# Last block of a fused GLA and RWKV-7 trunk: some scalings go from ACT and DVE to POOL, and the written-out order is another one

## The chip, the cores and the metric

The kernel runs on one core of a Trainium2 chip. The metric is the device time of one execution in microseconds. The core's engines are PE (TensorE; its weight loads are listed apart as PEld), DVE (VectorE), ACT (ScalarE) and POOL (GpSimd); SP (SyncE) issues the DMAs.

## The reference

One layer of a decoder trunk, batch 1, 4096 tokens, width 1024, all in float32. Cut to what matters:

```python
h = _rmsnorm(x, norm_w)
u = h @ w_in                                   # one input projection for both groups
gla_out  = rmsnorm_per_head(gla_chunked(q, k, v, log_a)) * gla_norm_w * silu(gg)     # 512 wide
rwkv_out = (groupnorm(rwkv7_scan(r, decay, k, v, kk, a)) * ln_w + ln_b + bonus) * silu(rg)   # 512 wide
merged = concatenate([gla_out, rwkv_out], axis=-1)          # 1024 wide
x = x + merged @ w_out
return _rmsnorm(x, final_norm_w)
```

The RWKV-7 recurrence is `S_t = S_{t-1} (diag(w_t) - kk_t^T (a_t kk_t)) + v_t^T k_t`, `y_t = S_t r_t`, for 8 heads of 64.

## The kernel before

**Tiling.** Everything is held transposed: features on the 128 partitions, tokens along the free axis. The 4096 tokens go in 8 blocks of `TB = 512`. A tensor of width 1024 is `KT = 8` row tiles of 128 x 512.

**Products in float16.** Each big product is made of float16 pairs: a scaled float32 tile becomes a high half (the scaled value rounded to float16) and a low half (what the rounding left). The weight is split in the same way, and three products are added in a bank of PSUM: high by high, weight high by low, weight low by high. `proj` writes that order; within it the row tiles go from 0 up, and the matmul of row tile 0 starts the bank. A step of PE that the code calls `both` is two matmuls, for the two halves of the output's partitions.

**Streams.** Generators emit the work of each stage for each block: the input norm, the weights' splitting, the RWKV preparation (a), its inverse (i), its chunk recurrence (c, and e for the very last unit), GLA (g), projections (p) and the output (o). They record 23,821 steps, each an instruction or a fixed pair with its engine, its data dependences and a number.

**The order is written out.** `ORDER` is a packed list with one rank for every step. The kernel issues the steps by rank, as far as the dependences allow (a heap of the steps whose predecessors are out), and this fixes each engine's own sequence, SP's queue of DMAs too. `STARTS` and `COUNTS` give every step a planned start, which decides how the streams interleave while the steps are recorded. Both lists were computed ahead of time and are data here.

**The last block's output, `out_last`.** Of the eight row tiles of the last merged block, the first six (`K0 = KT - 2`) are ready before the last two pairs of RWKV heads are. So the output projection of the six runs first:

- The largest absolute value of the six gives one scale, `am` (tile `oaml` in the profile).
- `scaled(k, a, ts)` makes the high half of row tile `k` on ACT into `mh[k][:, 0]` and the low half on DVE into `mh[k][:, 1]` (tiles `x` in the profile; their sources are `mgg` and `mgr`). The low half reads the high half.
- `proj(w, mh, "o", K0)` runs for each of the eight output row tiles `n`, with weights in `wr`, `wg` and `wo` in turn, three of them at a time on PE. DVE adds the residual into `part[n]`.

Meanwhile the last recurrence goes on: PE, ACT copies (`us`, `uv`, `gt`, `vt`) and DVE (`sv`) in a chain, between the projection's matmuls. The last two row tiles come in two halves of 256 tokens. For each half `i`: the two tiles are scaled, `last_mm` adds their products to `part[n]`, ACT squares it, PE sums the squares over features, DVE does a Newton iteration for the inverse root (`nva`, `nta`, `nyg`), PE spreads the result over the partitions, ACT copies it to `rb`, and each `part[n]` is multiplied by the final weight and that factor. For `n < 2` ACT multiplies by the weight beforehand and POOL by `rb`; for the others DVE does both in one instruction that reads the factor in PSUM. SP then stores each of the eight tiles, 128 KB each.

POOL's other work is the inverse of small triangular matrices (`Tc`, `tm`), sums of squares (`xacc`) and fills.

In the profile nearly all instructions carry the line of the helper that issued them (L849, or L910 for the paired matmuls), so steps are told apart by their tiles.

Of the kernel before, what the change touches and what calls it, by code (L numbers as in the profile page):

```python
# [17 lines left out]
U8 = mybir.dt.uint8  # L18
AF = mybir.ActivationFunctionType
ALU = mybir.AluOpType  # L20
# [4 lines left out]
P = 128  # L25
DM = 1024
KT = 8
TB = 512
TH = TB // 2
C = 64  # L30
# [12 lines left out]
DP = 0.15  # L43
DO = 0.3
SO = 0.3
DL = 0.6
# [11 lines left out]
    "c-q}v2bdjY)t)=IZ{KWsZzQBa5)vRFB!SSRBTYa-0Vx841qI}%hzJ&>SpWe+iedp3ML`6l7XkUD2}B?eY9N7-w!3%#Ihpr(-#z)J+}#cG{CS?q-FxrcnQy*wzH{F5o^!@~o|g%ZTyQ+y)zy{3``#Rl!SS)+2rkz("  # L58
    "Ab5Ql*ZoKES_zI~@OL&ie4O)fyvlbs2gk<2`~MAIHws=K3|{91uOow_Gx+<q;K<=V9l_rP{JkdlyM({xI$6^uy_cWR_UD6hT7%ai^ci1kaB$><<DHnk`VHD8?VX9w#-k1Lw><wT!Etr){h;9WNPPbN;QbD0=c%~<"
    "@ZgZ=nh+chqy3|T<E`NDrr=fj>hE~o8NqQU+CL3{OFQ}p$7{jgZD{|Z;O}zqIyE@Xr03`t9CePd)W7rS^E~yx{9SK8@1!v*(=~k@SseBFd;mV*GC1y`F>1i8%!5bK&hhAb`TdCC_%qIz`;EnQWv<*x&-DuamcD+I"  # L60
    "K9@e-0PWCr74Z8k&D&|1Q*u0B317d0{_^Sfa$Jnx9)sWR6C7^`f3L*6U*nj+Q>jg3g8xpY_t}K`+Arq2oa6T`HLm613Ewx#y32(3k$xGCK6IU1LVxG!v*zGf75wn4GU?@d^h_n1H!|*<<9WUsoPVy!23#*g^QElq"
    "!nNgIy9DR|E_i(|xW$RV>$mW#b7pby{Z^UkJ@*QZofBl?&|b>O4TEEA%$?_PFPYD+)GyjkB8!gh1KI3D7W9RT&(?VUV?p~j#owDjmOX)I@~M3yFWZC9CqSN6u!mG|?gfy0DqEV+ma$k{KKf0sRSJH%8uRnE;P`i?"
    "de8olCH*nyhSPHmr@0^XtViHp+oEkbTz4AgnC<%v#ygK|=BYn)f0~TzoE7{%ya(f3PI>MJ!S(y0t+Jnd5BqK%_6TXqX;{x0tm&bUjlU0$9nJGK^>7~5)83+cxBP3wK5_^8w-d5bzFUEN&rZ0u$hzs6Ynxziah<2~"
    "Y8uwR%%fSs>%W56<@j6fE3*7g!Rz)qFFM2V%9C#Km|xrT*Y(kQ)bam1&9x8n_(E`e7JaGr|3=V1j|Ba42-g4Q*q2Yj-1AAs%kdeRTfukJu(tjh{C#6^d@lHVN$`4;8NX%0`<5E!Sv|>yEXHg)zJD+H`%n1ppy2Ow"
    "g4dr1uips{)%9jVPVoAbYurz|XJ3t@>ImbY7ha9IB6`I2Mn4#7ey{p-t@kZs-x*4J(t*J-F*u$H-v2Z>-jBHMP&4ncSWnj^v||`##|JpC0nh0}4*57|GWJRN_mkk5NIIA5c0Ub{J<a_li7XC|Iq1uU!T0j|TqV9;"
    "#hCB%Df&`m#|dcP1;KHA@c#FZVcU`Jp|WR>;J<lj({||d>CkU$*@tuV`Ihv#+EKdCTob%L37zzb;J&*BuOjQN#ksq8g`fG3@$xap+VJ=4;M|Ylo`(c~Z)NmS)%SORd=lOGYr*SP!RsH<p3l*E%&1{a7h~qK9jk_z"
    "YssE641d2H(dSun?OOIXKBh*@vv$mnF~K3a(jKHA$#G1?J<i5?MXX;r7SQ*b<M(3Ui(L3Y@b^QoXY~5FC(N^klyYl*?JooH`g4a~wG5w$jMxPIum*Y~pL=rfz~^Mb{&}DDNFCcPg5#TX{hax|tk+kA??<H2e;Y8T"
    "RHtc-Id@=ih@SNl_P%AXZ++-Mosd~7BW3=bYW4s*_q1N<^78v{n|>YM$75Jb`2O%-USIa${ei3OQ%Se~*?oJpnO~(8<E($rgZw)S`g?}t;~kK5hX=<%`b{nNnC!oYVZKbndM=QhQ#r9M_PQIPlU_i&^~m7ZAO<gB"
    "omlmdm9WS7+}4CX@d<ZH>icPsc`QFhQX76_t}_n%`d9FLz8O3HY$){&V-iDfzr4W)f9a4JwH}2S{G--&@<1?P&*B;P$G+48nIQPV%hdLvuy?wkTW^TJABBGUM_f~EmoF1mSHw7Uk<4iz`KWsGAZp)UIPaF=^E!NA"
# [2122 lines left out]
```

## Time and profile before

| what | us |
|---|---|
| median of 3 runs | 2143.97 |
| lowest and highest run | 2140.78, 2145.99 |
| the profiled execution | 2141.45 |
| its span in the trace | 2139.7 |
| PE busy | 2092.8 |
| DVE busy | 1611.2 |
| ACT busy | 1276.9 |
| POOL busy | 898.7 |

The span is from the first instruction to the last; the execution's own time has 1.75 us around it. Busy time is a sum of instructions' durations; PE's are pipelined and their ends modelled, so starts are the safer thing to read on PE. A row of the timeline gives start, duration, engine, line, operation, `out<-in`, shapes and count, and in square brackets the engine's idle time before it with the work that ended it. Consecutive instructions of the same kind are merged into one row with their number behind the x.

### The profile page before, as it was taken

The numbers are of one execution on the slowest core, as the hardware profiler recorded it, in microseconds if no ns is written. First come the engines' busy times: TensorE is split into PE (matmuls) and PEld (weight loads), VectorE is DVE, ScalarE is ACT, GpSimd is POOL, SyncE is SP. The second block draws the span as 40 slices with busy tenths as digits, with TensorE's granted clock in tenths as the row PEclk, the third lists the DMA queues.
The fourth block names the chain that finished last, engine by engine and source line by source line (L and its number), as shares of the span: only waits on it lengthen the run. The fifth ranks groups of instructions, "written<-read, shape, count | busy, mean of one in ns | idle before, by whom it ended". The sixth has DMA issues, their size and how long they took to land. (4 is left out here: it accounts for less than half of the span.)

```text
span 2139.7 us, 69390 instructions
## 1 busy us (share of the span) xinstructions
PE 2092.8 (98%) x27936; PEld 1358.5 (63%) x27936; DVE 1611.2 (75%) x3531; ACT 1276.9 (60%) x3361; POOL 898.7 (42%) x2365
## 2 busy tenths in 40 slices
PE   7999999999999999999999999999999999999998
PEld 5656675666755657557576567656676565755566
DVE  8889988668775787678776776757877488676776
ACT  7678786465644656455755457545575465654563
POOL 3663344561353541636433264442434534444500
PEclk9999999999999999999999999999999999999999
DMA  6758656465344643455534554345634465444442
GB/s 177 232 154 260 212 176 184 129 193 169 93 132 130 200 142 113 122 152 181 150 98 123 168 177 142 105 127 184 180 99 118 135 189 164 112 109 137 140 126 90
DMA packets 273703, 322.33 MB, mean 151 GB/s; under 512 B 129844, under 2 KB 135140, under 8 KB 273380
## 3 DMA queue, kind: packets, MB, share of 16 engines
q1 hardware_dynamic: 273380, 317.89, 49.8%
q8 instruction: 219, 3.59, 0.7%
q14 instruction: 104, 0.85, 0.1%
HBM read 272.74 MB, written 45.05 MB: 149 GB/s over the span
## 5 line engine op out<-in xcount | busy, mean ns | idle before, releaser
L910 PE MATMUL bank<-x,wr 128*64 128x512 f16 (+1 forms) x6732 | 834.4, 379 | 3.0 <-ACT wr L849 1.5
L849 POOL TENSOR_TENSOR tm<-Tc,f 128x60 f32<-128x60 f32 (+24 forms) x961 | 330.0, 343 | 584.4 <-DMA f<-nd 511.4
L910 PEld LDWEIGHTS <-wr 128*64 128x64 f16 x6732 | 367.0, 111 | 258.2 <-issue 17.2
L910 PE MATMUL bank<-x,wg 128*64 128x512 f16 x3180 | 397.1, 380 | 2.0 <-DVE amW L849 1.4
L849 POOL TENSOR_TENSOR Tc<-Tc,tm 128x60 f32<-128x60 f32 (+24 forms) x961 | 361.6, 376 | 73.8
L910 PE MATMUL bank<-x,wo 128*64 128x512 f16 x2760 | 327.5, 380 | 0.0
L849 POOL TENSOR_TENSOR xacc<-xacc,xr 128x256 f32<-128x256 f32 x196 | 154.4, 813 | 317.4 <-ACT xr L849 193.9
L849 DVE SCALAR_TENSOR_TENSOR sv<-ch,PC,psd 64x64 f32<-64x64 f32 x434 | 122.6, 282 | 217.8 <-PE ch L910 193.0
L910 PEld LDWEIGHTS <-wg 128*64 128x64 f16 x3180 | 174.7, 110 | 130.7 <-issue 3.8
L910 PEld LDWEIGHTS <-wo 128*64 128x64 f16 x2760 | 150.3, 110 | 115.5 <-issue 1.2
L910 PE MATMUL bank<-wg,x 128*64 128x256 f16 x3072 | 197.6, 273 | 2.2 <-DMA wg<-wdr 2.0
L849 ACT COPY us<-ch 64x64 f32<-64x64 f32 x496 | 102.0, 206 | 146.8 <-PE ch L910 123.1
L910 PEld LDWEIGHTS <-x 128*64 128x64 f16 x3264 | 174.7, 110 | 15.5 <-DMA wg<-wdr 2.5
L849 ACT COPY uv<-ch 64x64 f32<-64x64 f32 x496 | 102.0, 206 | 93.1 <-PE ch L910 86.1
L849 ACT ACTIVATE psd<-sv,PC 128x128 f32<-128x128 f32 x248 | 98.7, 398 | 61.6 <-DVE sv L849 54.8
L849 ACT ACTIVATE sa<-bank,mu_s 128x512 f32<-128x512 f32 x104 | 71.3, 686 | 60.4 <-PE bank L910 52.0
L849 DVE COPY_PREDICATED DD<-mc,bank 64x512 f32<-64x512 uint8 x128 | 92.9, 729 | 4.4 <-PE bank L849 2.0
L849 DVE COPY_PREDICATED Nb<-mc,bank 64x512 f32<-64x512 uint8 x128 | 93.0, 730 | 3.3 <-PE bank L849 0.9
L910 PEld LDWEIGHTS ch<-us,Nb 128*64 128x64 f32 x992 | 66.4, 137 | 40.3 <-ACT us L849 10.8
L910 PEld LDWEIGHTS ch<-uv,bk 128*64 128x64 f32 x992 | 67.2, 137 | 38.7 <-ACT uv L849 5.7
L910 PEld LDWEIGHTS ch<-sv,DD 128*64 128x64 f32 x992 | 66.5, 137 | 35.6 <-DVE sv L849 9.3
L910 PE MATMUL ch<-us,Nb 128*64 128x64 f32 x992 | 71.6, 223 | 5.2 <-ACT us L849 5.2
(367 smaller groups left out, 3550.4 us busy)
## 6 DMA issues: line engine op xcount, KB each, us to landing
wr<-wdr SPq DMA_DIRECT2D x254, 256.0 KB
wg<-wdr SPq DMA_DIRECT2D x182, 256.0 KB
xr<-in_xT_dram SPq DMA_DIRECT2D x176, 256.0 KB
wo<-wdr SPq DMA_DIRECT2D x116, 256.0 KB
f<-nd SPq DMA_DIRECT2D x128, 128.0 KB
x<-in_wt_dram SPq DMA_DIRECT2D x29, 512.0 KB
wdr<-wo SPq DMA_DIRECT2D x17, 512.0 KB
rn<-bcda SPq DMA_DIRECT2D x64, 128.0 KB
```

The source lines that it names most:

```text
L849: put(t0, self.name, d, lag, cols, tiles, tab, outs, ins, lambda: f(*a, **kw))
L910: nc.tensor.matmul(x, lhsT=l, rhs=y, start=start, stop=stop)
```

## The change

Three things change.

1. In `scaled`, the high halves of row tiles 1, 3 and 5 of the first six are made by POOL with a `tensor_scalar`; the other highs stay on ACT, all lows on DVE.
2. In the final scaling, `n < 2` becomes `n < 2 + i`: in the second half (`i = 1`) three tiles go over ACT and POOL, and DVE has five. This makes one step more, 23,822.
3. `ORDER` is a new list. `STARTS` gains one entry and `COUNTS` counts it.

```diff
             def scaled(k, a, ts):
-                S.activation(mh[k][:, 0, ts], mgt[k][:, ts], AF.Copy, scale=am[:, a:a + 1])
+                if k < K0 and k % 2:
+                    G.tensor_scalar(mh[k][:, 0, ts], mgt[k][:, ts], am[:, a:a + 1], None, ALU.mult)
+                else:
+                    S.activation(mh[k][:, 0, ts], mgt[k][:, ts], AF.Copy, scale=am[:, a:a + 1])
                 V.scalar_tensor_tensor(mh[k][:, 1, ts], mgt[k][:, ts], am[:, a:a + 1], mh[k][:, 0, ts], ALU.mult, ALU.subtract)
...
                 for n in range(KT):
-                    if n < 2:
+                    if n < 2 + i:
                         S.activation(part[n][:, ts], part[n][:, ts], AF.Copy, scale=pkt[:, PK_FN + n:PK_FN + n + 1])
                         G.tensor_tensor(part[n][:, ts], part[n][:, ts], rb, ALU.mult)
                     else:
...
-COUNTS = (... ('o', 2545), ...)
+COUNTS = (... ('o', 2546), ...)
```

The packed list `ORDER` is left out of the diff. Decoded, the sequence of ACT around the first six highs is, before: uv, uv, gt, gt, high 0, vt, high 1, high 2, vt, high 3, high 4, us, us, high 5; after: uv, gt, gt, uv, high 0, high 2, vt, vt, high 4, us, us. POOL's new sequence there is high 1, high 3, high 5; DVE's lows go 0, 1, 2, 3, 5, 4 in place of 0, 1, 2, 4, 3, 5.

More of the change, by code (lines that the diff above doesn't have):

```diff
@@ new lines @@
+    "qmE0~Z4}<Wgmc%%n#jMu281fKdMfDL$DHZ!FTv|E!8y6$^<$v(6?m@Y!D}&iU4e1SI*g|=jSl`h-9cN~2wLk(pyzDD=Pe1pACd5Vmy9)2x#nnEH>Mfgn`6zM5;|QJOz4R+xuA&-d?&xj;oND#u@*i*IXM5^;PoNw"
+    "g(5z0!x(b7MhpJlIXM3p!Ryn(ElvzxzZ$%L9^VP?c`^8YyG*zTWe;p6>z2R^ht<g=g{G#1c3unaC3Dsu9Ljq-XwC+Lp6cbxzTssVTszaxhwDDVi#EdF<AdXc;Qd|T6MVjpxtWMHFGGgN{*%8i2j5fLZ6&%|jy+Yt"
+    "XR=14%i+YyoL(rjf_cniju!^++wu1Z8p~Ml3)l1I@j4GQv@Pzdv?@ILY{z=(dbZO3lh+w^&Ujqs>!69Y8t1(+<#`_j*YChsMJ8Mnyk7@%It=pYl;9W!nrs1|mhnCu96Orl8_-X*qw=PNab6!B2Y`R-K3|S|ubXhK"
@@ new lines @@
+    "0idA=gY&0Bwz%Yff%c^G=8eEF7U6H@4IrnL`bbYel<Q$#_47yk{@qJy*Hd55aOf-_#UXU^JItlZ%5wq*=x@R6{=sKI3SRFIUVjz5ei1r~eLk7fhd_s)3Xb0ff8P=uM?rtN)zI7`(m9fjX2_)i=^wqI3)NYE3!UxI"
+    ";J7IG`+LFb*PxHeIUCR($kKkl7kjn8<}z>ifyk?yuqTA}ucvv)L0{qDuOFeyrx{}#^xo&8uN(?q{1kZaq6j%O+OenPci&BrTSIXycAO`4@Lcfuw$Oi{1zlYl9HY!!jR}rjgX21L9a-Nq!DH8f9FqC@d$~4wny+yU"
+    "W!%RRt&~B_LhrLMKkXQ|oWEu8-`3@D&Ub<?KN@==Y40m7sxGbHO~vPOZ&|;|crSDKv*7jT!K={MUxE|%!hZS$_U{JJm3%`#S;)!J&>gZke-oVZN!UCcW}G?bRp$lAQNcMEK*s$B-yc%0=<Cz^VGoT?p#xjGSK0Gw"
@@ new lines @@
+    "!kiE6gFLgxRQkJQY*^KMJ`FypI>{*!eE$@TH;3nF01Yt@ku{%>{c{C)Rv9*meD<4uvi)5$xIeC=b99?yoD0FL#2%c4z1j(W!RK8TJn&~T;oj@Tvx{Cc4)*-a;PsrCd1$9KDy5)5u{&jdzlgbxqZ{=X<nhWn;c{Fj"
+    "gYV?^5<Ii|HL{SIY3V)c_(nhK4<q{Un@{xdUP{ON1+PB{UUw^pK7yp*S(*5uS^tI<_sw9x3N3v<cs(t6y`1*svf%GWKsytHV{?bUjIR}S$R3>ydHFiglTS9V{QYsz=k++}28{29;MgTNHcRjq<c<FMKAvS##GY`;"
+    "BpJ_}2|T5MebNXUMD9HZuWRCSSyR;^I&keK?C<lT&nvAiBcG2?GH8&w?-Z<S7xc<OxX)3JwW;-J#?c=((EY)pJqBOm-te~xA9xqG+xuRHm$lIPZ9p_4>n{Gt&w@Y7?{CC4dtpnL$TvEGWO|<VRWtFLxwzMzI7j!%"
@@ new lines @@
+    "hD66qL%$<B*v`=TKS&0xM|8}5|Bs|!FDKrZ$6OyAJf!$ieu4XlE^|b1Tphd@Ki~w+2h+wF%+I={$BcqqEZ_e#czrK{e$%Y;nh~GN`fU_k|L^2GlsTA<dwwNCN7)*-)(x<Ic7R^H(#IJbgW=OE&|1jf2a>L+>*ey%"
+    "tV4S+XP&hQ`shU12%F(t{qDlx#Fu(PKfa7@Q+$7B3LQ2R;p=E19d<e7oZ4NVz~{mXb^|Tv$Q~8H+E2h+E`<+apWyGqG1o_cK3Hb%Cj2<Kxaa~$_Ehs1%NrL2zZL)Pjll_<_EdZeS@Uc;$Nv6&@Y}0#?nLNgo#YFb"
+    "^L{Vy@yxyCKPzHibYiWi!xy4sodkOKq1*6%TOn^`?Zk)rx1Nd*pJ}=W`%>>+Ft+~opy9Ewb?yX@n1JtfETZR6!W=)2HPY*iGV}Bd(a8k*Zis^}{s7+7OFVnBIp+%UGZerR`1?y}ZiUXij&U52K(9mk!9V&G`4r^!"
@@ new lines @@
+    "7SJ%$&tS*?KZ3^4PV+nzHm*F2tjWH?aauXqj*&fdrR)V03v$`MLO+)W#|goCGFPX<p12NUm_hU+@3${kbRgAR7i2zKzf|Tw<PX#1=i=)Y8HK&2F*>2gYr8{UTCc7!-F)^)owi(u%K6}UHCV%AGNBB<2t20@*<<ys"
+    "UeX7eB6J$ouNx!u=`86rt)xfl8j22`%~bgDv*0Ub>|@rag;#!=-isc-9rlRYO>2QZ*(Pr_&o$OOOP=)pcA|Uc-<@P94kSHVjvay@ZUbMG=s?@!_a_mb=Vv}0`%}jF6#2F~an0YR@Iki6eAnuTB|bwspbuSrBJ5dt"
+    "{{x(NAn~omSPS);4tK<VdF@ZZTz(hhzY(t|2giI|Lv<CA7q1YFx%9DuvDwu3mW5oLhtG}xZRL%B!NoJy#P8(q&CTA*M$oy{4F{3z)-fF*K1;+k)_}d-VDwbc15d~J=V83oM=>a3KF$X(I0Syti)C-8;0>aq&%|7|"
@@ new lines @@
+    "8GC9O)_xYraT_Z=E_nY<{5=bCl(%qB5j=1Va1Y`mof~}d#h&o{M$&2S34Zf@!g%9o{%~4fvBxF8vx)Kh%bvJCSd6nVHa~&}vJP3CA#6vE_DLS&Qkl0E&iiHX-(JDJ&cb>|#TQ578sgWQ0v-QYv9Idj>v@W)sSe#~"
+    "zF$9u?3hKk4L$Z0{RNneWAK^yU@jmZNLt(3+I}*w3&CS8o<RTp9L}+FJ_}lFP2rmz<DjKoWX-^DK8?@BzjMQqa8F$m{Cxs+Y2lqSgZE3w_PQOqX#?r3N09IL=dewuV%)bv#^y2hM<Ey1!};gt-F%znrrMITFrU8-"
+    "HtYq3&^DL(ydikMUm@JfGN)$;?>8%iI(rFpy*ACC*p)jGU48|2`dIi12ATaa6`$!Gyqute=4;T`{D{5cL-&_^4l(pAJa#VDpcnC%9LauuT}ts`;RO?e_b<Voc^|Rx4`EZNO}(3AzxYJI1@QHSgj;awTLt=Ul1`{="
@@ new lines @@
+    "u9%{mvG;mmBhSY7_uzSbq9IG;f~C3?^t(Z?+h^K9xP^N4VewsweEBu@!YsswJ0KH<9_})8+JrU8g60@UHUfSp!R>tspU=iR4u>u%*ZgS=U)$6{hq_h|Ch)@zVT(26H+#}v7zuxkTzeq#Cws3AgZ~~ahx&-#_ek)X"
+    "mHtZjD0ip<FVI!T8jVkZ@9d_1<BHuj5v@vG@fO6X_Q3uV-`hcW-WjB$mEj{-oudbTPx=qpjjQ_@n(+O&OsGHf(!V=ags)p=Dwu%cYPNG<0X}!7Zzx!#T&AKgjHvV4MZ{b!&8qGze;<Z@CUo^BiDLjOvNb-xHo>k;"
+    ";~$VY-K8hwfoEpI{dOsMjL^9F;?E*|Sa?G@IB#%w82>&x(|2ElUh~s2_)WzHUTOAQGwBSXw~PIFQUc!^iRWq|pZfsl1ig?0Z#(YONdBEskPVwa|JoO8vJuwl`y}(kZV+DidhljNPiQA+h;J%wtAAio@ZUY%;qQO-"
@@ L366 @@
+    "Aqwt#KwHnkdxk*vyD<Wvbbr{Mxf*&=i?GA}Kc^=cG5"
 )
```

363 lines of the change are left out of this document (170 added, 193 removed).

## The prediction

> **What bounds the kernel now.** I read the page first: its busy shares say which engine to look at, and its slices whether that holds at all times.
>
> ```profile
> PE 2092.8 (98%) x27936; PEld 1358.5 (63%) x27936; DVE 1611.2 (75%) x3531; ACT 1276.9 (60%) x3361; POOL 898.7 (42%) x2365
> ```
>
> PE leaves 2139.7 - 2092.8 = 46.9 us of the span idle, and nothing but a part of that can be won while its work stays as it is. The view by stretches says where it lies (columns: stretch, length, then the busy time of PE, PEld, DVE, ACT and POOL with their instructions, PE's granted clock, DMA share, GB/s).
>
> ```profile
> 0.00:100.00 100.00, 82.44 (x962) 55.92 (x964) 85.43 (x235) 71.81 (x140) 47.78 (x102) 0.97 0.65 199
> 100.00:2000.00 1900.00, 1884.78 (x25084) 1213.57 (x25080) 1421.38 (x3001) 1135.31 (x3014) 827.60 (x2218) 1.00 0.51 151
> 2000.00:2040.00 40.00, 36.35 (x512) 26.49 (x509) 32.82 (x74) 20.28 (x55) 20.51 (x44) 1.00 0.41 125
> 2070.00:2080.00 10.00, 8.24 (x96) 4.91 (x94) 7.87 (x22) 9.52 (x30) 0.00 (x0) 1.00 0.77 199
> 2080.00:2124.00 44.00, 44.00 (x686) 31.29 (x683) 26.84 (x87) 15.97 (x54) 0.00 (x0) 1.00 0.21 67
> ```
>
> The change touches 2070 to 2080 (idle 10 - 8.24 = 1.76 us) and what comes after 2124. Between them PE is busy 44.00 of 44 us, so whatever PE gains before 2080 moves the end by as much, and an ACT or DVE step made shorter there gains nothing by itself. In the chain that ended last, the first stretch shows who holds PE back.
>
> ```profile
> 2073.56 0.73 ACT x L849
> 2074.33 0.41 PE bank L910 x2
> ...
> 2074.90 0.85 ACT x L849 x2
> ...
> 2076.00 1.34 ACT x L849 x2
> ...
> 2077.82 0.73 ACT x L849
> 2078.60 2.03 PE bank L910 x20
> ```
>
> The x rows are the high halves of the six row tiles, all made by ACT. The first releases PE at 2074.33, the last at 2078.60; from 2078.60 the chain stays on PE. POOL does nothing in that time, and ACT is busy for 9.52 of the ten microseconds.
>
> **The first edit: three highs on POOL.** ACT's highs cost 718 ns each; between them stand the copies of the last recurrence.
>
> ```profile
> L849 ACT ACTIVATE x<-mgg,oaml 128x512 f16<-128x512 f32 x4 | 2.8, 718 | 0.1
> ...
> 2072.65 0.42 ACT L849 COPY uv<-ch 64x64 f32<-64x64 f32 x2
> 2073.10 0.44 ACT L849 COPY gt<-bank 64x64 f32<-64x64 f32 x2
> ...
> 2075.77 0.21 ACT L849 COPY vt<-bank 64x64 f32<-64x64 f32 x1
> ```
>
> Three leave ACT: 3 x 0.718 = 2.15 us of ACT time. They are row tiles 1, 3 and 5. The first matmul of every bank takes row tile 0 (only it carries the start flag), so PE cannot begin before ACT's first high. Decoded, the new ranks keep that high behind the same two uv and two gt copies. I therefore leave the 2074.33 where it is. PE's rows say what is lost behind it.
>
> ```profile
> 2074.33 0.41 PE L910 MATMUL bank<-x,wr 128*64 128x512 f16 x2 [0.41 <-ACT x L849]
> ...
> 2074.88 0.41 PE L910 MATMUL bank<-x,wo 128*64 128x512 f16 x2
> 2075.19 0.41 PE L910 MATMUL bank<-x,wg 128*64 128x512 f16 x2
> ...
> 2076.48 0.31 PE L910 MATMUL bank<-vt,bk 128*64 128x64 f32 x4
> 2076.78 0.41 PE L910 MATMUL bank<-x,wr 128*64 128x512 f16 x2
> ...
> 2078.23 0.28 PE L910 MATMUL bank<-sv,DD 128*64 128x64 f32 x4
> 2078.60 0.62 PE L910 MATMUL bank<-x,wr 128*64 128x512 f16 x4
> ...
> 2080.32 0.31 PE L910 MATMUL bank<-gt,Nb 128*64 128x64 f32 x4
> 2080.43 0.31 PE L910 MATMUL ch<-uv,bk 128*64 128x64 f32 x4
> ```
>
> Ends of matmuls are modelled, so I use starts. Four small f32 matmuls hold PE for 2080.43 - 2080.32 = 0.11 us when something is ready; at 2078.23 they hold it for 0.37, because the sixth high is still being made. That is 0.26 us lost to ACT. The group of four at 2076.48 holds it for 0.30, another 0.19 lost; and the two matmuls at 2074.88 hold it for 0.31 where the chain's 2.03 us for twenty give 0.20 for two, 0.11 lost. Together 0.56 us behind the first high. With three highs from POOL the sixth row tile is there before PE asks, and ACT's vt pair, whose second copy starts at 2075.77, moves ahead of ACT's third high, about 0.6 us earlier. What is late next is ACT's first high, then the low halves on DVE.
>
> POOL's price is not in the trace: it makes no scaling with a per-partition factor. The nearest rows:
>
> ```profile
> L849 POOL CAST smask<-xr 128x512 uint8<-128x512 f32 x1 | 0.6, 633 | 1.9 <-DMA xr<-in_ck_dram 1.9
> ...
> L849 POOL TENSOR_TENSOR xacc<-xacc,xr 128x256 f32<-128x256 f32 x196 | 154.4, 813 | 317.4 <-ACT xr L849 193.9 <-ACT xacc L849 83.0 <-PE ch L910 21.1
> L849 POOL TENSOR_TENSOR mgg<-mgg,rk 128x256 f32<-128x256 f32 x4 | 2.8, 728 | 105.6 <-ACT rk L849 105.6
> ...
> 2072.70 0.21 DVE L849 TENSOR_SCALAR oaml<-pw 128x1 int32<-128x1 int32 x2
> 2074.32 0.75 DVE L849 SCALAR_TENSOR_TENSOR x<-mgg,oaml,x 128x512 f16<-128x512 f32 x1 [0.16 <-ACT x L849]
> ```
>
> One input over 512 elements: 0.63 us by the cast, and at most 0.81 x 2 = 1.63 us if each 256 elements cost as much as the two-input sum. I take 0.7 us, the cast being the same shape. The factor is there at 2072.70 + 0.21 = 2072.91, and POOL waits for nothing else, so its highs land near 2073.6, 2074.3 and 2075.0 (at the upper price 2074.5, 2076.2 and 2077.8, the last still ahead of the 2078.55 at which ACT delivers the sixth today). The new wait of POOL for the factor holds up nothing: behind it on POOL stand only the products after 2124.
>
> DVE makes the low halves from the highs, so three of them now wait for POOL. They lie beside each other and may slow each other. From below the cost is nothing; from above, DVE's lows of the first three row tiles wait out POOL's second and third high in full, 2 x 0.7 = 1.4 us, and hand it on to PE. I take nothing: PE takes lows only after the highs of the six row tiles in a bank.
>
> In sentences of their own: the Trainium skill, "SBUF — State Buffer", section "Who interferes with whom", says that a DVE instruction with two SBUF inputs and a GpSimd instruction that reads SBUF exclude each other for their whole length. The trace agrees only in part: POOL's product of 256 elements is 728 ns in the quiet tail, and the sum of the same shape, made among DVE's work, 813 ns on average. By that rule the lows and POOL's highs would run one after the other, which is the 1.4 us above; I carry it as a rival.
>
> So the first edit: between -1.76 (all idle of the ten microseconds) and +1.4 us; taken -0.4, most of the 0.56 us that the starts show lost behind 2074.33.
>
> **The second edit: a third scaling of the second half on ACT and POOL.** DVE makes five scalings in place of six; ACT gets one more multiply by the weight and POOL one more product.
>
> ```profile
> 2131.44 0.16 DVE L849 SCALAR_TENSOR_TENSOR nyg<-nva,nyg 128x2 f32<-128x2 f32 x1
> ...
> 2133.56 0.33 SPq L849 DMA_DIRECT2D out_dram<-mgg  x1
> ...
> 2136.97 0.40 SPq L849 DMA_DIRECT2D out_dram<-mgr  x1
> ...
> 2133.05 0.48 DVE L849 SCALAR_TENSOR_TENSOR mgg<-mgg,pkt,bank 128x256 f32<-128x256 f32 x1 [1.06 <-ACT rk L849]
> 2133.10 1.41 POOL L849 TENSOR_TENSOR mgg<-mgg,rk 128x256 f32<-128x256 f32 x2 [6.29 <-ACT rk L849]
> ...
> 2134.63 0.86 DVE L849 SCALAR_TENSOR_TENSOR mgr<-mgr,pkt,bank 128x256 f32<-128x256 f32 x2
> ```
>
> DVE's last scaling ends at 2134.63 + 0.86 = 2135.49; with one fewer, at about 2135.1. POOL's third product would end at 2133.10 + 3 x 0.705 = 2135.2. All eight tiles are ready 0.3 us sooner, but the stores do not follow: SP issues eight of them from 2133.56 to 2137.37, one every 3.81 / 8 = 0.48 us, slower than DVE, whose second scaling starts 0.86 - 0.47 = 0.39 us after its first. SP's queue sets the end, and it starts with DVE's first tile as before. In the new ranks it takes POOL's first product second and POOL's second product third; the latter is ready at 2134.51, where the third issue would be due at 2133.56 + 2 x 0.48 = 2134.52. So gain 0, loss up to 0.1. The added ACT multiply has 1.4 us until POOL asks for it, and ACT has no other work left after its copy of the spread factor. The second product's multiply now stands behind that copy too, with 0.7 us to go. Three scalings of the first half stand behind the Newton steps on DVE in the new ranks (they end at 2131.44 + 0.16 = 2131.60 today) and would end near 2132.9, before the second half begins at 2133.05; if that cover went, the stores would slip by up to 0.3. Taken +0.1, range 0 to +0.3.
>
> **The third edit: the order.** The planned starts are equal for all 23,821 steps that both versions have. The ranks are not: laid against the steps, 1,216 of PE's 12,992 (9.4%) leave their place among the rest, 798 of DVE's 3,531, 703 of ACT's 3,210, 491 of 1,729 DMA issues, but no step goes further than 92 places on PE. These are small swaps over the whole span, and no row shows their price. I bound it by the idle time that they can make or take: 17.56 + 15.22 + 3.65 = 36.4 us from the stretches before 2040, times 9.4%, is 3.4 us either way. I take 0, for lack of a row that favours a sign.
>
> **Sum.** -0.4 + 0.1 + 0 = -0.3 us on the profiled execution's own 2141.45 us (span 2139.7 and 1.75 around it): 2141.15. The median of the runs shown is 2143.97, 2.5 us (0.12%) above that execution, so on that scale 2143.7.
>
> **The rivals.** *The lock between DVE and POOL:* the 1.4 us above in place of -0.4, so 2143.97 + 1.5 = 2145.5. For it: 813 against 728 ns. Against: PE has highs to work on. Still not a measurable change.
>
> *The order wins in the start-up.* PE's waits in the first 100 us:
>
> ```profile
> PE bank L910 <- ACT rk L849: 3.6, 1, 3.6
> PE bank L910 <- ACT wo L849: 3.6, 3, 1.8
> ```
>
> If the new order took both, 7.2 us, the time would be 2136.5. It decides only from 6.4 us on, so nearly both must go. Against it: of DVE's steps in the start-up only two memsets and a few one-column steps move, and the Newton steps keep their places.
>
> *The order makes a weight late* (slower). SP issues all DMAs in one row, and 491 of them moved. One such wait is in the trace:
>
> ```profile
> PE bank L910 <- DMA wg<-wdr: 2.0, 1, 2.0
> ```
>
> Each further one costs 2.0 us as PE has no spare time to make it good; the fourth decides: 2143.7 + 8 = 2151.7. Against it: in 1900 us of the middle no wait of PE names a DMA, so the landings have slack there.
>
> *The change does not do what it says:* POOL's highs come, but PE waits for ACT's first high alone and the 0.56 us stays: 2143.97 + 0.1 = 2144.1, inside the forecast.
>
> **How the numbers follow.** A measurement of this kernel tells about 0.3%, 6.4 us, from no change. No measurable change 0.90: the forecast (with the case that nothing is gained) 0.80 and the lock 0.10. The start-up win 0.06, the late weights 0.04. Faster by over 0.3%: 0.06; within: 0.90; slower: 0.04. The range takes the forecast with the order's 3.4 us and the runs' own spread (2140.78 to 2145.99, -3.2 and +2.0 around the median): root of squares 4.7 down and 3.9 up, so 2139.0 to 2147.6. The lock lies inside; the other two rivals, 0.10, are left out.
>
> **What would show it.** In the changed kernel's trace: POOL rows x<-mgg and x<-mgr of some 0.7 us from 2072.9 on; ACT's first high still at about 2073.6 and PE's first matmul on it near 2074.3; the four small matmuls before the last high no longer hold PE for 0.37 us; PE busy 44 of 44 us up to the tail; eight stores at 0.48 us each, ending no sooner after the first. I am wrong if PE's idle time before 2000 differs by more than 3.4 us, if DVE's lows begin after PE asks for them, or if the last store follows the first by less than 3.3 us.

## The result, and the profile after

The changed kernel is slower: 2152.83 us in the median of seven runs (2149.5 to 2156.93) against 2143.97 for the kernel before (2140.78 to 2148.0). The ratio of the two is 1.0034, with a 95% interval from 1.0019 to 1.0049, so about 7 us. The forecast was 2143.7 in a range up to 2147.6, with 0.04 for a loss of over 0.3%.

The profiled execution of the changed kernel took 2154.63 us with a span of 2152.8. That is 13.2 us more than the profiled execution of the kernel before, so these two traces show more than the 7 us of the medians. First the page's line of busy times, then the view by stretches (columns as in the prediction), with the stretches moved by what the kernel has fallen behind: 2083 to 2093 holds the six highs, as 2070 to 2080 did.

```profile
PE 2093.5 (97%) x27936; PEld 1360.5 (63%) x27936; DVE 1606.6 (75%) x3530; ACT 1273.8 (59%) x3359; POOL 918.2 (43%) x2369
```

```profile
0.00:100.00 100.00, 81.55 (x968) 54.70 (x970) 86.39 (x235) 70.95 (x141) 46.96 (x104) 0.98 0.67 205
100.00:2000.00 1900.00, 1874.48 (x24924) 1209.45 (x24922) 1409.24 (x2982) 1126.18 (x2988) 835.13 (x2191) 1.00 0.50 150
...
2083.00:2093.00 10.00, 7.49 (x88) 4.72 (x90) 7.65 (x20) 5.92 (x21) 6.28 (x3) 1.00 0.77 208
2093.00:2137.00 44.00, 44.00 (x682) 31.45 (x680) 26.86 (x86) 16.59 (x57) 0.00 (x0) 1.00 0.19 64
```

PE has the same work (2093.5 us against 2092.8). The loss is idle time, and it lies far from the edited code: between 100 and 2000 us PE idles 1900 - 1874.48 = 25.5 us where it idled 15.2. The stretch of the six highs gave away 2.51 - 1.76 = 0.75 us. So the first suspect is the new order, which reaches the middle.

To place it I matched DVE's instructions of two traces by operation, tiles, shape and number of occurrence, and took the median difference of their starts within 20 us of a point. This is how far a kernel has fallen behind the kernel before (us; e1 to e16 are the experiments below; small differences come from the start-up and vary between runs):

| kernel | at 430 | 500 | 730 | 950 | 1270 | 1350 | 2090 |
|---|---|---|---|---|---|---|---|
| changed kernel | 0.6 | 3.4 | 3.4 | 7.8 | 8.0 | 12.8 | 13.2 |
| e1, new order alone | -1.1 | 1.5 | 1.5 | 5.1 | 5.8 | 7.9 | 7.9 |
| e2, both edits, old order | 0.6 | -0.1 | 0.1 | 0.1 | -0.1 | 0.6 | 2.3 |
| e3, highs on POOL, old order | -0.6 | -0.5 | -0.5 | -0.5 | -0.7 | 0.0 | 0.2 |
| e12, old order, one step moved | -0.4 | 2.6 | 2.7 | 2.7 | 2.4 | 3.1 | 2.0 |
| e13, new order but two stretches | -0.1 | -0.1 | 2.4 | 2.6 | 2.8 | 4.4 | 4.2 |
| e14, old order, stretch 1 new | 0.6 | 3.9 | 4.0 | 4.0 | 4.4 | 4.9 | 4.2 |
| e15, old order, stretch 2 new | 2.8 | 2.4 | 2.9 | 6.0 | 5.8 | 6.1 | 7.3 |
| e16, second half new | 0.1 | 0.2 | 0.4 | 0.8 | 1.0 | 3.7 | 4.2 |

In the changed kernel and in e1 the loss is made in three places, with little between them: near 467 us (2.6 to 2.8), near 776 (3.6 to 4.4) and near 1300 (2.1 to 4.8; the old orders lose 0.6 to 0.7 there too). At the first, the timeline of the changed kernel's ACT and PE reads:

```profile
465.44 0.40 ACT L848 ACTIVATE psd<-sv,PC 128x128 f32<-128x128 f32 x1
469.30 0.63 ACT L848 ACTIVATE xr<-xr 128x512 f32<-128x512 f32 x1 [3.45 <-DMA xr<-in_xT_dram]
469.95 0.42 ACT L848 COPY uv<-ch 64x64 f32<-64x64 f32 x2
...
470.43 0.34 PE L909 MATMUL ch<-uv,bk 128*64 128x64 f32 x4 [2.22 <-ACT uv L848]
```

ACT squares a tile of x for the next block's norm (`xr<-xr`, in `x_block`). Its load is late, and the copies `uv` of the recurrence, which have their operand, stand behind it in ACT's queue. PE waits 2.22 us for them. In the kernel before, the timelines of ACT and PE have the same late load, with the copies ahead of it:

```profile
463.98 0.42 ACT L849 COPY uv<-ch 64x64 f32<-64x64 f32 x2
464.43 0.78 ACT L849 ACTIVATE ta<-bank,half_p,lrs 128x512 f32<-128x512 f32 x1
467.40 0.63 ACT L849 ACTIVATE xr<-xr 128x512 f32<-128x512 f32 x1 [2.19 <-DMA xr<-in_xT_dram]
...
465.31 0.31 PE L910 MATMUL ch<-uv,bk 128*64 128x64 f32 x4
```

ACT waits 2.19 us there too, and PE does not notice: its row for the same product has no wait.

### The profile page after: what moved, and what is told of

Read it like the earlier page. It is cut to its first block, busy times and chain, and to the rows that moved or that the text cites. A ratio compares the mean times of both kernels' runs of the same rounds, so it can differ in the third digit from the quotient of the medians.

```text
span 2152.8 us, 69381 instructions
## 1 busy us (share of the span) xinstructions
PE 2093.5 (97%) x27936; PEld 1360.5 (63%) x27936; DVE 1606.6 (75%) x3530; ACT 1273.8 (59%) x3359; POOL 918.2 (43%) x2369
## 4 chain that ended last, share of the span: by engine, by line
PE 72%; DVE 9%; POOL 7%; DMA 5%; issue 3%; ACT 2%; SPq 1%; POOLq 0%; DVEq 0%; ACTq 0%
PE bank L909 57%; PE bank L848 9%; PE ch L909 4%; POOL Tc L848 3%; POOL tm L848 3%; DVE DD L848 1%; PE y L848 1%; PE y L909 1%; SPq L848 1%; DMA xr<-in_xT_dram 1%; DVE bk L848 1%; DMA f<-nd 1%; DMA wg<-wdr 1%; DVE nva L848 1%; DVE x L848 1%
## 5 line engine op out<-in xcount | busy, mean ns | idle before, releaser
L848 POOL TENSOR_TENSOR tm<-Tc,f 128x60 f32<-128x60 f32 (+24 forms) x961 | 352.0, 366 | 572.0 <-DMA f<-nd 500.9
L848 POOL TENSOR_TENSOR Tc<-Tc,tm 128x60 f32<-128x60 f32 (+24 forms) x961 | 353.1, 367 | 74.0
L909 PE MATMUL ch<-uv,bk 128*64 128x64 f32 x992 | 72.1, 224 | 4.5 <-ACT uv L848 4.5
```

Of the source, the lines that this page charges most:

```text
L848: put(t0, self.name, d, lag, cols, tiles, tab, outs, ins, lambda: f(*a, **kw))
L909: nc.tensor.matmul(x, lhsT=l, rhs=y, start=start, stop=stop)
```

## The experiments

### Which of the three edits

Theory A: the order costs, the code edits do not. Rival B: POOL's highs cost, by the lock with DVE. Each run keeps a part of the change. All of them are compared in runs on one chip with the kernel before.

```diff
 e1: before.ORDER = the new list, without the rank of the added step
 e2: all edits, ORDER = the old list with a rank put in for the added step
 e3: the old list; only the edit in scaled():
+                if k < K0 and k % 2:
+                    G.tensor_scalar(mh[k][:, 0, ts], mgt[k][:, ts], am[:, a:a + 1], None, ALU.mult)
 e4: the old list; only the edit of the last scalings:
-                    if n < 2:
+                    if n < 2 + i:
```

> The kernel before, with the new order alone (the one added step taken out of the list). Theory A, the searched order itself is slow away from the last block: about 2152, some 8 us above the kernel before, with PE waits of 1 to 3 us at a handful of places in the middle. Theory B, POOL's high halves and the third scaling make the loss: 2144, no difference.

> Both code edits with the old order (one rank put in for the added step). Theory A: 2144 to 2146, at most 2 us above the kernel before, the part that POOL's highs of 2 us each cost. Theory B: about 2152.

> The first edit alone with the old order: POOL makes three highs. Theory A: +1 to +2 us, with a PE wait of about 1.4 us on a POOL high near 2076, POOL's highs 1.5 to 2.4 us each. Theory B: +8. By the prediction's price of 0.7 us a high: -0.4 us.

> The second edit alone with the old order: five scalings on DVE, three products on POOL in the second half. Theory A: within 0.3 us of the kernel before, the stores still 0.48 us apart and the last one as late. Theory B: part of the 8 us.

| run | median us | ratio to before (95%) |
|---|---|---|
| before | 2144.61 | |
| e1, order alone | 2152.46 | 1.0030 (1.0017 to 1.0043) |
| e2, both edits, old order | 2144.5 | 0.9999 (0.9985 to 1.0013) |
| e3, highs on POOL | 2146.29 | 1.0002 (0.9989 to 1.0015) |
| e4, third scaling | 2145.04 | 0.9999 (0.9984 to 1.0015) |

The order alone makes the loss; the two code edits together change nothing that shows in the time. For e3 1 to 2 us were expected, and its 0.4 us can't be told from nothing. Rival B falls for the time, though the price of the highs was well off: from the groups of POOL's instructions by shape (ns, shortest, median and longest) of the changed kernel,

```profile
L848 POOL TENSOR_SCALAR x<-mgg,oaml x2: 1567/2382/3197, 2085.4 to 2086.9; 128x512 f16<-128x512 f32 x2
L848 POOL TENSOR_SCALAR x<-mgr,oaml x1: 1557/1557/1557, 2090.1 to 2090.1; 128x512 f16<-128x512 f32 x1
```

and of e3:

```profile
L849 POOL TENSOR_SCALAR x<-mgg,oaml x2: 1569/1730/1892, 2073.8 to 2075.3; 128x512 f16<-128x512 f32 x2
L849 POOL TENSOR_SCALAR x<-mgr,oaml x1: 1559/1559/1559, 2077.2 to 2077.2; 128x512 f16<-128x512 f32 x1
```

A high takes 1.56 us at the least, and 3.20 us for the changed kernel's second one. Beside that one DVE makes three lows without a pause, and PE then waits for it; the timeline of the changed kernel:

```profile
2086.64 2.06 DVE L848 SCALAR_TENSOR_TENSOR x<-mgg,oaml,x 128x512 f16<-128x512 f32 x3
...
2090.18 0.41 PE L909 MATMUL bank<-x,wr 128*64 128x512 f16 x2 [1.40 <-POOL x L848]
```

The high starts near 2086.9, within the first low; the lows end at 2088.70, and 1.43 us later the high is done. By the exclusion in the Trainium skill, "SBUF — State Buffer", section "Who interferes with whom", which the prediction put as a rival, a high that starts during a low waits for its end. Here the trace agrees, and it shows that the high got in only after the third low, not between two. In e3 DVE's lows come one at a time beside the second high, it takes 1.89 us, and PE waits for none of the highs.

### By engine and by half

Theory A (second set): the loss is made on SP, whose loads of x stand behind issues that wait. Theory B: by what stands ahead of what on the computing engines. Theory C: by the fit of the engines' orders to each other. Both lists are kept, and each step takes its rank from one of them:

```diff
-        rank = order()
+        rank, new = order(ORDER), order(ORDER_NEW)
+        for s in steps:
+            if CONDITION:
+                rank[s.n] = new[s.n]
 e5: s.eng == "D"   e6: s.eng != "D"   e7: s.eng == "T"
 e8: max(rank[s.n], new[s.n]) < 11900
```

> The kernel before, in which only SyncE's transfers take their place in the emission from the new order; PE, DVE, ACT and POOL keep the old one. The new order alone cost 7.9 us (2152.46 against 2144.61). Theory A (the loss is made on SP: the loads of x stand behind issues that wait, such as the write td<-Tc, so they land late): 2150 to 2153, and in the stretch 100 to 2000 us the waits of ACT and DVE for the transfer xr<-in_xT grow from 4.2 and 3.7 us to over 7 each. Theory B (the loss is made by what stands ahead of what on the computing engines; the transfers only follow): 2143.5 to 2145.5, the xr waits as before. Theory C (no engine's order is at fault, only its fit to the others'): also slower, since this kernel mixes the two orders; it is told from A by the next run.

> The counterpart: PE, DVE, ACT and POOL take the new order, SyncE's transfers keep the old one. Theory A: 2143.5 to 2146, with the idle of PE between 100 and 2000 us back at about 15 us (25.5 in the changed kernel, 15.2 before). Theory B: 2151 to 2153, idle 22 us or more. Theory C (fit): slower in both mixed kernels, each by 4 us or more.

> Only TensorE's steps take the new order, all other engines keep the old one. If the loss is in PE's own sequence (part of theory B: a product stands ahead of others and waits for an operand that comes late): 2150 to 2153, and the waits of PE are the ones of the changed kernel (for ACT uv, DVE sv, ACT x). If it is in the order of DVE, ACT and POOL, or on SP (A): 2143.5 to 2146. Theory C: 2149 or more.

> The new order on all engines for the first half of the steps (those whose place is below 11900 of 23821 in both orders, to about 1080 us), the old one for the rest. Where the loss is of the places seen in the trace of the changed kernel (+1.6 us by 200 us, +2.2 at 475, 3.9 by 820, 5.3 by 1300, 9 by the last block): 2148 to 2149. Where it is made late, in the second half (the order alone showed +2.4 at 775 and +7.9 at the end): 2144.5 to 2147. Where it is one place in the first half that decides: 2151 to 2153.

| run | median us | ratio to before (95%) |
|---|---|---|
| before | 2143.35 | |
| e5, SP new | 2149.0 | 1.0028 (1.0018 to 1.0037) |
| e6, all but SP new | 2160.17 | 1.0083 (1.0069 to 1.0096) |
| e7, PE new | 2183.98 | 1.0193 (1.0179 to 1.0207) |
| e8, first half new | 2150.87 | 1.0028 (1.0015 to 1.0041) |

Theory C is the one that stands: every mixture by engine is slower, and two of them by far more than the new order itself. Theory A falls: in e5 the waits of ACT and DVE for loads of x grow from 4.2 and 3.7 us to 5.3 and 5.0, not to over 7 each, and e6, which has SP's old order, is slower still. In these mixtures an engine's sequence is good only beside the others it was computed with, so these three runs can't tell where the loss sits. Cut by time the order can be taken apart: the first half alone costs 6.0 us (3.2 to 8.8).

### Single steps at the two first places

At 776 us the timelines of POOL and SP show how the second place comes about. In the kernel before:

```profile
749.85 0.61 POOL L849 TENSOR_TENSOR tm<-Tc,f 128x49 f32<-128x49 f32 x1
750.55 0.29 POOL L849 TENSOR_TENSOR Tc<-Tc,tm 128x49 f32<-128x49 f32 x1
...
753.89 0.38 SPq L849 DMA_DIRECT2D xr<-in_xT_dram  x1
...
755.73 0.59 POOL L849 TENSOR_TENSOR Tc<-Tc,tm 128x8 f32<-128x8 f32 x1
...
756.35 0.37 SPq L849 DMA_DIRECT2D td<-Tc  x1
...
760.90 0.35 SPq L849 DMA_DIRECT2D xr<-in_xT_dram  x1
```

and in e1, the new order alone, with PE's waits behind it:

```profile
754.06 1.84 POOL L850 TENSOR_TENSOR tm<-Tc,f 128x49 f32<-128x49 f32 x1
755.98 1.85 POOL L850 TENSOR_TENSOR Tc<-Tc,tm 128x49 f32<-128x49 f32 x1
...
764.24 0.22 POOL L850 TENSOR_TENSOR Tc<-Tc,tm 128x8 f32<-128x8 f32 x1
764.49 0.38 SPq L850 DMA_DIRECT2D td<-Tc  x1
...
765.54 0.43 SPq L850 DMA_DIRECT2D xr<-in_xT_dram  x1
...
772.85 1.27 PE L850 MATMUL bank<-ident,bk 128*128 128x128 f32 x8 [0.89 <-DVE Nb L850]
775.04 1.70 PE L911 MATMUL bank<-x,wr 128*64 128x512 f16 x14 [0.34 <-DMA wr<-wdr]
777.08 1.49 PE L911 MATMUL bank<-x,wr 128*64 128x512 f16 x12 [0.34 <-ACT x L850]
```

POOL's chain for the triangular inverse ends at 764.46 instead of 756.32 us, 8.1 us later, of which 1.5 us had been lost earlier. SP can't issue `td<-Tc` before it, and in the new order a load of x that went out ahead of that write (753.89) now stands behind it (765.54). PE waits for nothing between 700 and 900 us in the kernel before, and in e1 for DVE, a weight and ACT in turn. Part of the delay lies in POOL's own products: the two of 128x49 take 1.84 and 1.85 us in e1 and 0.61 and 0.29 in the kernel before, which is 2.8 of the 6.6 us that are new here. DVE runs full-width operations beside them in both kernels, so what makes them long in one is not shown.

Theory Q: what costs is who stands behind an instruction that waits. It is tested by single moves: one step of ACT at 467 us (e9), three issues of SP at 756 us (e10), both (e11), and the reverse in the kernel before, one step of 23,821 (e12). The expectations call the step of ACT a scaling; it squares.

```diff
 new order, in order():
+    r[4999] = 5264.5                                             # e9, e11: xr<-xr behind uv, uv, gep, ta
+    r[9072], r[8173], r[8177] = 8503.3, 8503.4, 8546.5           # e10, e11: wg, xr ahead of td<-Tc; xr ahead of two Nb<-td
 old order:
+    r[4999] = 5242.5                                             # e12: xr<-xr ahead of uv, uv, ta
```

> The new order alone (7.9 us slower), with one step of ACT put back: the scaling xr<-xr of x near 467 us, which waits for its load, goes behind the two copies uv<-ch, gep and ta that the new order had put behind it (the old order has it behind them too). Theory Q (a queue head: the load lands at about 467.3 us in both orders, and what costs is who stands behind the instruction that waits for it): the idle of PE between 300 and 500 us falls from 3.2 to 3.6 us to 0.8 to 1.8, the wait for ACT's uv of 2.0 to 2.2 us goes; time 1.5 to 3 us below the new order's 2152.5. Theory L (the stretch loses because the loads land late, whoever waits): the idle moves to another reader and stays above 3 us; time as the new order's, 2151 to 2154.

> The new order alone, with three issues of SyncE near 756 us put back as in the old order: a weight load (wg) and a load of x go ahead of the write td<-Tc, which waits for POOL until 764.5 us (756.4 in the kernel before), and the next load of x goes ahead of two reads Nb<-td. Theory Q (what stands behind the waiting write pays): the loads issue near 757 us, DVE's waits for xr<-in_xT near 771 to 776 us shrink from 2.4 us to under 1, and the idle of PE between 700 and 900 us falls from 2.2 to 3.4 us to under 1.3; time 1.5 to 3 us below 2152.5. Rival R (the lateness of POOL's chain itself decides, by way of td, Nb and the products behind them): the idle stays at 2 us or more, and PE's wait is then for Nb, Ta or DD instead of x or wg.

> Both repairs at once, four steps of 23821. Theory Q: the idle of PE is under 1.8 us in 300 to 500 us and under 1.3 in 700 to 900 us, and the time falls by 3 to 6 us below the new order's, to 2146.5 to 2149.5 (the kernel before 2144). If the two places are only the largest of many small losses, no more than 2 us come back: 2150.5 to 2152.5. If the places trade one delay for another further on (the gain is given back by 1300 us): 2151 to 2153 with both stretches mended.

> The kernel before, with one step of 23821 moved: the same scaling xr<-xr of ACT goes ahead of the two copies uv<-ch and ta near 464 us, as in the new order. Theory Q: PE waits for uv about 2 us near 467 us, the idle between 300 and 500 us grows from 0.8 to 2.5 to 3.6 us, and the time is 1.5 to 3 us above the kernel before (2145.5 to 2147). Theory L or slack later on: 2143.5 to 2145, the idle under 1.5 us.

| run | median us | ratio to before (95%) |
|---|---|---|
| before | 2142.9 | |
| e9, place 1 mended | 2150.41 | 1.0032 (1.0022 to 1.0043) |
| e10, place 2 mended | 2150.78 | 1.0031 (1.0019 to 1.0043) |
| e11, both mended | 2150.54 | 1.0031 (1.0020 to 1.0042) |
| e12, old order, one step ahead | 2146.88 | 1.0012 (1.0001 to 1.0023) |

e12 agrees with theory Q: one step put ahead of two copies and one more step costs 1.0012 x 2142.9 - 2142.9 = 2.6 us (0.2 to 4.9), and the kernel falls behind by 3.0 us between 430 and 500 and by nothing more to 1270. Its PE:

```profile
467.05 0.34 PE L911 MATMUL ch<-uv,bk 128*64 128x64 f32 x4 [1.92 <-ACT uv L850]
```

The repairs gave nothing back, which theory Q did not expect. In e9 the wait at 467 us is gone, but the next square but one takes its place (timelines of ACT, then PE), and PE idles 2.85 us between 300 and 500 us where it idled 3.20 in e1. That is nearly what its rival, theory L, expected (over 3 us, at another reader):

```profile
463.54 0.43 ACT L851 COPY uv<-ch 64x64 f32<-64x64 f32 x2 [0.27 <-PE ch L912]
...
466.71 0.63 ACT L851 ACTIVATE xr<-xr 128x512 f32<-128x512 f32 x1 [1.77 <-DMA xr<-in_xT_dram]
...
472.20 0.63 ACT L851 ACTIVATE xr<-xr 128x512 f32<-128x512 f32 x1 [2.01 <-DMA xr<-in_xT_dram]
472.85 0.42 ACT L851 COPY uv<-ch 64x64 f32<-64x64 f32 x2
...
473.33 0.34 PE L912 MATMUL ch<-uv,bk 128*64 128x64 f32 x4 [2.07 <-ACT uv L851]
```

In e10 the load goes out at 757.10 as meant, but POOL's chain is as late as ever (`td<-Tc` at 763.58), and PE now waits 1.38 us for a weight `wr` behind that write; its idle between 700 and 900 us is 2.49 us against e1's 2.22. Of the expectations, rival R came nearest for e10, without the operand that it named. In e11 the time is that of its second expectation, but neither stretch is mended (PE idles 3.37 and 4.77 us in the two). So in these runs a repair of the first queue head uncovers the second.

### Whole stretches, and the loads of x

Is the loss local to these stretches, or only visible there? All engines get the old or the new order inside them. Stretch 1 is places 4300 to 5800 (about 390 to 520 us), stretch 2 is 7600 to 9000 (690 to 815 us).

```diff
 CONDITION, with lo <= min(rank, new) and max(rank, new) < hi for a stretch:
 e13: not (stretch 1 or stretch 2)   e14: stretch 1   e15: stretch 2
 e16: min(rank[s.n], new[s.n]) >= 11900
```

> The new order, but all engines keep the old order in two stretches: the steps with places 4300 to 5800 and 7600 to 9000 in both orders (about 390 to 520 and 690 to 815 us), 2878 of 23821 steps. Theory local (the loss is made by the order within these stretches; the new order alone lost 2.4 to 2.8 us of PE time between 300 and 500 us and 2.2 to 3.4 between 700 and 900 us): both stretches idle under 1.3 us, time 2 to 4.5 us over the kernel before instead of 8. Theory spread (any place of the new order is tight, the stalls only show up there): as with the single steps put back, 6.5 to 8 us over it, the idle turning up elsewhere.

> The old order, with the new one on all engines in the first stretch alone (places 4300 to 5800, about 390 to 520 us). Theory local: PE's idle between 300 and 500 us is 2.5 to 3.6 us instead of 0.8, with the wait for ACT's uv near 467 us, and the time 2 to 3.5 us over the kernel before. Theory spread: under 1.5 us of idle, time within 1.5 us of it.

> The old order, with the new one on all engines in the second stretch alone (places 7600 to 9000, about 690 to 815 us). Theory local: POOL's chain Tc ends near 764 us instead of 756, the loads of x behind td<-Tc go out after it, PE idles 2 to 3.5 us between 700 and 900 us instead of 0, and the time is 2 to 3.5 us over the kernel before. If what decides is when POOL's chain starts and what DVE does beside it, set by the order ahead of the stretch: POOL ends near 757 us, idle under 1 us, time within 1.5 us of the kernel before.

> The counterpart of the first half: the new order only for steps with places from 11900 on in both orders (from about 1080 us). The first half alone cost 6.0 us by the ratio (1.0028), the whole order 7 (1.0033). If the two halves add up: 0 to 2.5 us over the kernel before. If the second half of the new order has its own loss that its first half hid: 4 us or more over it.

| run | median us | ratio to before (95%) |
|---|---|---|
| before | 2144.03 | |
| e13, new order but two stretches | 2147.12 | 1.0011 (1.0001 to 1.0022) |
| e14, stretch 1 new | 2148.08 | 1.0021 (1.0009 to 1.0033) |
| e15, stretch 2 new | 2149.28 | 1.0019 (1.0010 to 1.0029) |
| e16, second half new | 2147.63 | 1.0017 (1.0008 to 1.0026) |

Much of it is local. With the old order in 2,878 of the 23,821 steps, the new order keeps 2.4 us of its 6.4 (the ratios times 2144). The intervals of the two overlap (0.2 to 4.7 and 3.6 to 9.2); the table of the traces says it better, with 4.3 us lost between 430 and 2090 in e13 and 9.0 in e1. Each stretch of the new order alone costs the old one 4.5 and 4.1 us, a little above what was expected. What e13 keeps sits at its seam after stretch 1 (2.5 us between 500 and 730) and near 1300. The two halves, 6.0 and 3.6 us, add up to 9.6 against 6.4 to 7.3 for the whole; their intervals cover that, and e16's 3.6 lies between its two expectations. The view by stretches shows PE's 200 us windows of the kernel before,

```profile
300.00:500.00 200.00, 199.22 (x2642) 127.33 (x2640) 152.53 (x319) 114.97 (x311) 91.00 (x234) 1.00 0.53 160
700.00:900.00 200.00, 200.00 (x2702) 131.41 (x2700) 151.85 (x312) 117.25 (x317) 88.53 (x235) 1.00 0.49 146
```

of e13,

```profile
300.00:500.00 200.00, 199.14 (x2638) 127.01 (x2636) 152.63 (x319) 114.19 (x311) 93.43 (x234) 1.00 0.53 159
700.00:900.00 200.00, 200.00 (x2685) 130.85 (x2682) 154.18 (x315) 117.61 (x317) 87.87 (x236) 1.00 0.50 146
```

and of the changed kernel:

```profile
300.00:500.00 200.00, 196.47 (x2612) 125.67 (x2608) 148.18 (x312) 114.27 (x312) 92.69 (x234) 1.00 0.53 161
700.00:900.00 200.00, 196.96 (x2614) 129.34 (x2612) 152.68 (x316) 117.54 (x316) 89.92 (x220) 1.00 0.48 143
```

PE idles 0.78 and 0.00 us in the kernel before, 0.86 and 0.00 in e13, 3.53 and 3.04 in the changed kernel. In e15 `td<-Tc` goes out at 765.90, although everything before 690 us has the old order. In e14, which has the old order there, it goes out at 760.42, later than the kernel before only by the 4.0 us that it is behind at 730. So POOL's lateness is made inside the second stretch.

The last pair asks whether late loads of x are the common cause. In both orders they are cut to 128 of 512 columns; the other columns keep what the buffer held, so these two kernels no longer compute the layer.

```diff
-                D.dma_start(xr, xT[P * k:P * k + P, TB * b:TB * b + TB])
+                D.dma_start(xr[:, 0:P], xT[P * k:P * k + P, TB * b:TB * b + P])
...
-                    S.activation(xr, xr, AF.Square)
+                    S.activation(xr, xr, AF.Square, scale=0.001)
...
-            y = newton(ps[:, 0:P], 1.0 / DM, 1e-6, None, "g")
+            y = newton(ps[:, 0:P], 1e6 / DM, 1.0, None, "g")
...
-                D.dma_start(t, xT[P * k:P * k + P, TB * b:TB * b + TB])
+                D.dma_start(t[:, 0:P], xT[P * k:P * k + P, TB * b:TB * b + P])
```

> The kernel before (old order), with the loads of x for the normalization of each block cut to 128 of 512 columns, both times that x is read (left out: the other columns, whose buffers keep old values; the squares are scaled by 1e-3 and the mean by 1e6 so that these stay finite, and three buffers are set once at the start). The number of instructions and transfers and the order stay. Serves as the base for the next run. Theory X (late loads of x are what the stalls have in common): 0 to 4 us under the kernel before, since its own waits for x between 100 and 2000 us, 7.9 us on ACT and DVE, mostly are not on PE's path; either way within 5 us of it.

> The new order alone, with the same cut of the loads of x as the run before. Theory X: the difference between the new and the old order, 7 to 8 us with whole loads, shrinks to 0 to 3 us with the small ones, and the idle of PE at 467 and 776 us is under 1 us each. Rival (the loads only show the wait; what is late is the freeing of their buffers, POOL's chain, or the queue ahead of them on SyncE): 5 to 8 us stay, with the waits for uv near 467 us and for x or a weight near 776 us in place.

The kernel before took 2142.55 us beside them; e17 took 2142.64 (ratio 1.0004, 0.9993 to 1.0014) and e18 2145.04 (1.0012, 1.0002 to 1.0022). The difference of the orders shrinks from 6.4 us (e1) to (1.0012 - 1.0004) x 2143 = 1.7 us, 2.4 by the medians. ACT's and DVE's waits for loads of x between 100 and 2000 us fall from 10.0 us in e1 to 3.6 in e18. So theory X has a part of the loss, and how large a part stays open. The intervals of these ratios are 4 to 6 us wide, as wide as what shrank. PE still idles 2.25 us between 300 and 500 us in e18, not under 1, with a wait of 1.1 us for `uv`, and matched as above e18 falls 4.6 us behind e17 in their two profiled executions, where e1 fell 7.9 behind the kernel before. Smaller loads also leave the queues more room for everything else, weights included, and no run here parts the two.

Why the loads can be late at all stands in SP's waits between 455 and 470 us (us in total, times, the longest), in the kernel before and in e1:

```profile
SPq L849 <- POOL xacc L849: 7.0, 3, 4.3
```

```profile
SPq L850 <- POOL xacc L850: 9.3, 2, 6.8
```

Tiles of x pass through three buffers (`NXR = 3`). A load is issued only when POOL's sum (`xacc`) has read the buffer's last contents, and that sum follows ACT's square. ACT, POOL and SP so form a ring through three engines' queues. A square placed early on ACT waits for the ring, as at 467 us; that a late one holds it up is argued, not shown. A fourth buffer was not tried.

The third place, near 1300 us, was not tested beyond e16, which has it with the old order up to 1080 us. In the trace of the changed kernel it looks like the second. SP waits for POOL's chain, `td<-Tc` goes out at 1288.38 (10.8 us later than in the kernel before, of which 8.0 had been lost earlier), loads of x stand behind it, DVE waits for them, ACT for DVE, and PE for ACT (SP's waits between 1275 and 1300, then the timelines of SP, DVE and PE):

```profile
SPq L848 <- POOL Tc L848: 8.2, 1, 8.2
...
1291.57 0.87 SPq L848 DMA_DIRECT2D xr<-in_xT_dram  x2
...
1295.43 0.75 DVE L848 SCALAR_TENSOR_TENSOR xr<-xr,nwx,xacc 128x512 f32<-128x512 f32 x1 [2.29 <-DMA xr<-in_xT_dram]
...
1296.88 0.41 PE L909 MATMUL bank<-x,wr 128*64 128x512 f16 x2 [1.32 <-ACT x L848]
1299.04 1.92 PE L909 MATMUL bank<-x,wr 128*64 128x512 f16 x8 [1.75 <-ACT x L848]
```

In e1, which loses less there, PE's longest wait is 1.40 us for DVE's `sv`.

No version beat the kernel before.

## Why the prediction was wrong

**The step that failed is the third edit: the order, taken at 0 and bounded by 3.4 us.** It cost 6.4 us alone (e1; 3.6 to 9.2 by its interval). Three things were wrong in that step. The bound took PE's present idle time as what an order "can make or take". For a gain that is a bound; for a loss it is not, since PE's idle is then made anew out of the slack of the other engines. The share was PE's 9.4%, while at the places traced the loss came by way of ACT, SP and POOL; on ACT 22% (703 of 3,210) and on SP 28% (491 of 1,729) of the steps had moved. And "small swaps" were taken to be worth little each: e12 shows one, past three steps of ACT, that is worth 2.6 us. The row that would have warned was there: ACT's wait of 2.19 us for a load of x at 467.40, with an operand of PE just ahead of it. The prediction looked at which waits PE had, not at which waits of other engines had work for PE next in line. What makes POOL's products and the ring late in the new order stays open.

**The rival "the order makes a weight late"** had the right sign and nearly the right time (2151.7), and 0.04. The time was luck: it counted four waits of 2.0 us for weights, and weights are not what PE mostly waited for. A DMA issued late is a cause at the second place; at the first, the load lets ACT start at 467.40 us in the kernel before and 467.31 in e1, and ACT's sequence makes the loss. PE's own waits for weights in the changed kernel:

```profile
PE bank L909 <- DMA wg<-wdr: 2.6, 3, 1.5
PE bank L909 <- DMA wr<-wdr: 0.3, 1, 0.3
```

Together 2.9 us against 2.0 before. Between 100 and 2000 us its longest sums of waits are for ACT's `x` (4.5 us) and `uv` (3.7) and DVE's `sv` (3.6), against 1.4 for weights, so "no wait of PE names a DMA" was the wrong thing to lean on.

**The first edit** (taken -0.4) had its price mis-sized, 0.7 us for 1.56 alone and up to 3.20. The cast was not the near row; two sums of 256 elements (1.63) were. In e3 the last high lands 2078.75 - 2073.62 = 5.1 us after the factor is there, where that price had given 4.9 and the price taken 2.1. The gain came even so, with the old order. PE's starts, matched as above within 2.5 us, lie 0.71 us behind the kernel before's at 2072 and 0.21 at 2084 in e3, and 2.83 and 2.33 in e2: 0.50 us won in both, where 0.56 was counted as lost behind the first high. Four kernels with the old order there and the highs on ACT (e4, e12, e14, e17) keep their distance within 0.02 us. PE's idle time hides the gain (10 - 8.31 = 1.69 us between 2070 and 2080 in e3, 1.76 in the kernel before), since the ends of matmuls are modelled, and a time within 0.15% can't show it.

**The rival of the lock** was put at 1.4 us, and PE's wait for POOL in the changed kernel is 1.40. That the numbers agree is chance: the rival had DVE's lows wait for two highs of 0.7 us, and what happened is that a high of 1.56 us waited for DVE's lows. In e3 no wait of PE came of it.

**The second edit** (taken +0.1, range 0 to +0.3) can't be told from nothing by the time (e4: 0.9999). In the traces e4 is 2.97 us behind at 2120 and 3.20 at the end, e2 2.33 and 2.64: 0.2 to 0.3 us later, though other tails vary by 0.2 as well. So the two code edits did about what their terms said, and the sum failed by the order. **The start-up win** did not come: PE idles 18.45 us in the first 100 where it idled 17.56, and no run here has it under 14.6. **PE's 44.00 of 44 us** after the highs held. The prediction named the test that it fails, PE's idle before 2000 within 3.4 us: it grew by 0.9 + 10.3 = 11.2 us in the profiled execution.

## What to carry to other kernels

A new order is an edit of its own: run it alone and the code edits under the old order, before anything is read into either. To see what an order risks, list the instructions on every engine that wait for a DMA, and look at what stands behind them for the bound engine; in e12 the loss was at least the whole wait, on an engine that had hardly been idle there. Here single steps put back mended nothing, since the next queue head took over, while stretches with all engines' orders put back together mended both places. And a gain of half a microsecond can be read from matched starts where neither idle time nor run times show it.

## What the hardware showed that was not expected

- POOL's multiply by a per-partition factor, 128x512 float32 to float16, takes 1.56 us; the cast of the same shape to uint8 takes 0.63.
- A POOL product of 128x49 took 1.84 us in e1, and one of 128x54 a little earlier 0.62; the kernel before has that product of 128x49 at 0.61. DVE's full-width operations run beside all of them.
- PE's busy time for the same 27,936 matmuls ran from 2092.1 us (e17) to 2107.2 (e7) over the profiled executions, with the mean granted clock at 0.996 and 0.992. The clock's 0.4% would account for an estimated 8.4 of these 15.1 us. So a part of a slower kernel's time can sit in PE's busy time rather than in its idle time: e1's span is 7.9 us longer than that of the kernel before, and only 2.8 us of that is idle time, with the clock at 0.993 against 0.996.
